# q computed transposed and unnormalised, with the root of its mean square moved into the scale of the sigmoids

## The chip, the cores and the metric

The kernel runs on one core of a Trainium2 chip, as one launch. The metric is the device time of that launch in microseconds (us). A core has a matrix engine (TensorE: PE, with its weight loads shown as PEld), a vector engine (VectorE: DVE), a scalar engine (ScalarE: ACT), a general engine (GpSimd: POOL) and a synchronisation engine (SyncE: SP), on which this program issues nearly all of its DMAs. Each engine works through its own list of instructions in order.

## The reference, cut to what matters

One layer of a streaming encoder, for 2048 tokens of width 1024. What touches the change is the attention branch: q, k and v are projections of the normalised input, q and k are normalised per head (8 heads of 64), and the scores' sigmoid is what the stick-breaking weights are made of.

```python
h = rms_norm(x, norm_g) * (1.0 + scale) + shift
u = h @ w_in
glu_in, gate_a, q, k, v, gate_b, m_a, m_b = jnp.split(u, IN_SPLITS, axis=-1)
...
q = q * lax.rsqrt(jnp.mean(q * q, axis=-1, keepdims=True) + EPS) * q_gain   # per head of 64
k = k * lax.rsqrt(jnp.mean(k * k, axis=-1, keepdims=True) + EPS) * k_gain
...
z = jnp.einsum("bqhd,bkhd->bhqk", qb, kb) * 64 ** -0.5
beta = sigmoid(z)                       # and 1 - beta = sigmoid(-z)
A[t, s] = beta[t, s] * prod_{s<j<t} (1 - beta[t, j])                        # s < t
o = A @ v
```

The other branch (a gated causal convolution of width 31 with a layer norm) and the gates, the output projections and the residual are the same before and after.

## The kernel before, in words

**Number format.** Every large product is made of three matmuls (`mm3`): each fp32 operand is split into a rounded part hi and a rest lo, and hi·hi, hi·lo and lo·hi are summed in PSUM.

**Stages.** The sequence is handled in 4 chunks of 512 tokens, in the order 3, 2, 1, 0 (the host has reversed it). The program has four stretches.

1. The opening (0 to about 166 us). The modulation columns are computed on DVE and ACT, x is loaded, normalised and transposed on PE into h^T (8 tiles of 128 channels by 512 tokens per chunk, hi and lo), chunk after chunk. The first chunk's q, k and v are computed here "at once", with weights and staging tiles out of a pool `hx` that lives only in the opening. SP's list in it holds the loads of w_ada, of the q, k and v weights and of x, and the stores of q, k and v, mixed.
2. The projections (to about 775 us): the other three chunks of q (group 0, then, after some gates, group 1), k and v; the GLU and the gates for all four chunks. A group is four heads. The convolution's taps are on a list `todo`, from which a few are emitted at each `tick()`; work that has to wait for other engines is put off by `later(n, ...)`, which runs it n ticks on.
3. The attention (to about 1520 us): 80 units (8 heads, and 10 pairs of a row chunk with a key chunk), each with four blocks of 128 queries. For each block: two z matmuls into PSUM, on ACT a sigmoid of z into w and one of -z back into z, on DVE a scan that multiplies up the sigmoids of -z, on POOL the product w. One unit later PE transposes w (four at a time), ACT copies the hi part and DVE subtracts the lo part, and PE multiplies by v. Between these, PE does the merge gates' matmuls as filler, at due times.
4. The output projections (to the end).

**Order.** The scheduler orders the instructions of each engine up to the end of q's group 0. From then on `pin[0]` is set, and PE's instructions (`mm`, `tr`) keep the order in which the program writes them, until the end of the attention.

**q and k before.** `nat_mm` (L215) takes h^T, 128 channels by 128 tokens, as the stationary operand and 256 columns of weights as the moving one: the result is q as tokens by channels, two such blocks in one PSUM tile `pd`, a half (two blocks) being 48 matmuls of 256 columns. ACT squares each head with an accumulator (L297; in the opening one Square for the half at L356 and a sum on DVE at L358). `head_norm` (L305) makes the root by three Newton steps on DVE and multiplies q by it into `qn` (L312). `transposed` (L318) turns `qn` on PE, four transposes for two heads (L123), into the PSUM tile `pt`; ACT writes hi (L331, for k with its gain L327), DVE lo (L332), and four DMAs on SP store them (L336, L337). The tiles `qhi` and `qlo` have one buffer each. k goes the same way with its own weights. In the attention `load_q` (L940) fetches q^T with three DMAs; `z_stage` (L948) multiplies and applies both sigmoids with the constants 1/8 and -1/8 as scale (L970, L971); `av_stage` (L991) transposes.

Of the kernel before, what the change touches and what calls it, by code (L numbers as in the profile page):

```python
# [8 lines left out]
F32 = mybir.dt.float32  # L9
# [42 lines left out]
def trunk_kernel(  # L52
# [105 lines left out]
    qst_d = [[dram(f"qst{h}_{g}", [P, CH], F32) for g in range(NCH)] for h in range(NH)]  # L158
    vst_d = [[dram(f"vst{h}_{g}", [P, 4, P], F32) for g in range(NCH)] for h in range(NH)]
# [40 lines left out]
    with ExitStack() as s1:  # L200
# [81 lines left out]
        def qk_group(grp, isk, chunks, w2=None):  # L282

            w2 = w2 or [piece(w_qkv[grp, i]) for i in range(2)]
            h4 = (grp % 2) * 4
            dst = kst_d if isk else qst_d
            for b in chunks:
# [14 lines left out]
                for pr in range(2):  # L302
                    later(3 + pr, lambda qn=qn, b=b, pr=pr: transposed(qn, pr, dst, h4, b, isk))
# [14 lines left out]
        def transposed(qn, pr, dst, h4, b, isk, pool=None):  # L318
# [5 lines left out]
            hi = (pool or cvp).tile([P, CH], F32R, tag="qhi", name="qhi", bufs=1)  # L324
            lo = (pool or cvp).tile([P, CH], F32R, tag="qlo", name="qlo", bufs=1)
            if isk:
                nc.scalar.mul(hi, ps, gain)  # L327
                nc.vector.scalar_tensor_tensor(out=lo, in0=ps, scalar=gain, in1=f(hi),
# [4 lines left out]
            for i in range(2):  # L333
                hd = slice(i * HD, (i + 1) * HD)
                dd = dst[h4 + 2 * pr + i][b]
# [14 lines left out]
        def norm_at_once(pss, grp, b, pool):  # L350
# [11 lines left out]
            for pr in range(2):  # L362
                transposed(qn, pr, kst_d if grp >= 2 else qst_d, (grp % 2) * 4, b, grp >= 2, pool)
# [36 lines left out]
        def h_chunk(g, pool, on_dve, xs=None, parts=4):  # L400
# [7 lines left out]
            for kc in range(KC):  # L408
# [3 lines left out]
                hf = pool.tile([P, CH], F32, tag="hf", name="hf", bufs=6)  # L412
# [8 lines left out]

        with tc.tile_pool(name="hx", reuse_waits="tile", bufs=1) as hx:
# [10 lines left out]
            def hf_tile():  # L433
                return hx.tile([P, CH], F32, tag="hf", name="hf", bufs=6)
# [30 lines left out]
            crow = [hx.tile([P, CH], F32, tag="hf", name="crow", bufs=6)[0:1] for _ in range(2)]  # L465
# [31 lines left out]
            qk_ps = [[pd.tile([P, 2, 256], F32, tag="pd", name="pd") for _ in range(2)]  # L497
# [13 lines left out]
            for kc in range(KC):  # L511
# [46 lines left out]

# [739 lines left out]
```

## Time and profile before

| what | value |
|---|---|
| time, median of 3 runs | 1840.88 us (1836.46 to 1841.89) |
| the profiled execution | 1840.99 us, its span 1839.3 us, granted clock 0.998 |
| busy over the span: PE, DVE, ACT, POOL | 1777.6, 1233.2, 833.5, 658.7 us |

| stretch (us) | length | PE busy | DVE busy | ACT busy | POOL busy |
|---|---|---|---|---|---|
| opening, first part, 0 to 20 | 20 | 6.66 | 9.06 | 7.99 | 0.75 |
| q of the first chunk, 20 to 55 | 35 | 30.23 | 29.49 | 21.40 | 3.18 |
| rest of the opening, 55 to 166 | 111 | 100.06 | 68.92 | 65.11 | 44.23 |
| projections, 166 to 775 | 609 | 606.51 | 435.36 | 163.99 | 128.73 |
| attention, 775 to 1520 | 745 | 720.94 | 571.00 | 537.51 | 466.34 |
| output projections, 1520 to 1839 | 319 | 313.19 | 119.42 | 37.48 | 15.44 |

The span is what the profile sees between its first and last instruction; the time has 1.7 us more around it. A busy time counts an engine's instructions as they overlap in its pipeline, once. In the lines of the trace, L12 is line 12 of the kernel, `x4` is a count, and an arrow `<-` at the end of a row says which work ended the idle time before it.

### The profile page before, as it was taken

To read this page: it belongs to the slowest core of one execution; us is meant where nothing else is said; L and a number is where in the kernel's file an instruction comes from. 1 tells how busy PE (TensorE), PEld (TensorE's weight loads), DVE (VectorE), ACT (ScalarE), POOL (GpSimd) and SP (SyncE) were. 2 spreads that over 40 slices of the span, in tenths; PEclk is the share of its full clock that TensorE was granted. 3 is DMA by queue.
4 is the path that set the end of the run, shared out by engine and by line. 5 is a ranking of instruction groups with operands and counts; after the bars stand their busy time and mean duration, and the time that the engine had idled before them with its cause. 6 is when DMAs were issued, how large, how long until landed. Compare 5 with 4: busy or idle time off the path is not lost.

```text
span 1839.3 us, 27219 instructions
## 1 busy us (share of the span) xinstructions
PE 1777.6 (97%) x9612; PEld 1510.2 (82%) x9612; DVE 1233.2 (67%) x1696; ACT 833.5 (45%) x1960; POOL 658.7 (36%) x819
## 2 busy tenths in 40 slices
PE   6899999999999999999999999999998899999999
PEld 5888889899898888878888888888776777888887
DVE  7645577987879565467778777877778785334341
ACT  5465113223131234367777777777777742010100
POOL 0253112102111233366666666666666721010100
PEclk9999999999999999999999999999999999999999
DMA  8563411415133453433232323232334336353532
GB/s 288 177 188 105 139 35 53 120 42 168 33 104 98 152 182 132 152 117 98 61 107 66 106 72 101 67 95 66 95 111 137 95 110 203 109 166 97 166 97 81
DMA packets 117597, 211.08 MB, mean 115 GB/s; under 512 B 15442, under 2 KB 27730, under 8 KB 117460
## 3 DMA queue, kind: packets, MB, share of 16 engines
q1 hardware_dynamic: 116308, 207.24, 36.2%
q10 hardware_dynamic: 1152, 2.10, 0.3%
q8 instruction: 76, 1.25, 0.3%
q14 instruction: 61, 0.50, 0.1%
HBM read 137.98 MB, written 71.30 MB: 114 GB/s over the span
## 4 chain that ended last, share of the span: by engine, by line
PE 75%; DVE 7%; DMA 5%; POOL 4%; issue 4%; ACT 4%; SPq 1%; DVEq 0%; ACTq 0%; POOLq 0%
PE pd L118 43%; PE po L118 8%; PE p L118 8%; PE av L118 5%; PE pT L123 5%; PE z L118 5%; POOL w L982 2%; DVE sc L975 2%; DVE tlo L1009 1%; DMA wl<-in_w_qkv_dram 1%; ACT z L971 1%; POOL wlo L106 1%; PE pt L123 1%; DMA qst<-qhi 1%; DMA xt<-in_x_n_dram 1%
## 5 line engine op out<-in xcount | busy, mean ns | idle before, releaser
L982 POOL TENSOR_TENSOR w<-w,sc 128x512 f32<-128x512 f32 (+1 forms) x320 | 361.3, 1130 | 243.0 <-DVE sc L975 177.5
L118 PE MATMUL pd<-hh,whi 128*128 128x512 f32 x1024 | 325.8, 399 | 0.0
L975 DVE TENSOR_TENSOR_SCAN sc<-z,sc,w 128x512 f32<-128x512 f32 x192 | 244.1, 1276 | 73.8 <-ACT z L971 72.2
L106 POOL TENSOR_TENSOR wlo<-wl,whi 128x512 fp32r<-128x512 f32 x88 | 130.9, 1499 | 409.4 <-ACT whi L105 408.4
L970 ACT ACTIVATE w<-z 128x512 f32<-128x512 f32 (+1 forms) x320 | 171.6, 536 | 128.9 <-PE z L118 102.9
L118 PEld LDWEIGHTS pd<-hh,whi 128*128 128x128 f32 x1024 | 184.2, 190 | 31.4
L118 PE MATMUL pd<-hhi,whi 128*128 128x512 f32 x512 | 208.5, 407 | 1.0 <-ACT vsg L882 1.0
L1009 DVE TENSOR_TENSOR tlo<-pT,thi 128x512 fp32r<-128x512 f32 (+1 forms) x320 | 185.8, 598 | 33.6 <-ACT thi L1008 30.5
L118 PE MATMUL pd<-hh,wlo 128*128 128x512 f32 x512 | 200.3, 391 | 0.0
L118 PE MATMUL pd<-hhi,wlo 128*128 128x512 f32 x512 | 200.2, 391 | 0.0
L118 PE MATMUL pd<-hlo,whi 128*128 128x512 f32 x512 | 200.2, 391 | 0.0
L118 PE MATMUL z<-kt,q 128*128 128x512 f32 (+2 forms) x640 | 190.5, 379 | 0.0
L123 PE MATMUL pT<-ident,w 128*128 128x128 f32 x1088 | 174.3, 274 | 11.9 <-POOL w L982 10.4
L1008 ACT CAST thi<-pT 128x512 fp32r<-128x512 f32 (+1 forms) x320 | 165.1, 526 | 42.6 <-PE pT L123 38.7
L123 PEld LDWEIGHTS pT<-ident,w 128*128 128x128 f32 x1088 | 136.8, 140 | 50.6 <-POOL w L982 18.6
L971 ACT ACTIVATE z<-z 128x512 f32<-128x512 f32 (+1 forms) x320 | 171.8, 537 | 0.0
L979 DVE TENSOR_TENSOR_SCAN sc<-z,tri 128x512 f32<-128x512 f32 (+3 forms) x128 | 103.9, 820 | 60.3 <-ACT z L971 40.6
L118 PE MATMUL av<-tlo,vt 128*128 128x512 f32 (+1 forms) x320 | 121.0, 378 | 11.1 <-DVE tlo L1009 10.4
L105 ACT CAST whi<-wl 128x512 fp32r<-128x512 f32 x88 | 53.6, 622 | 163.2 <-PE pd L118 135.5
L118 PEld LDWEIGHTS z<-kt,q 128*128 128x128 f32 x640 | 109.6, 189 | 14.6 <-DVE sc L979 0.3
L118 PE MATMUL av<-thi,vt 128*128 128x512 f32 (+1 forms) x320 | 116.7, 365 | 0.8 <-ACT thi L1008 0.8
L1116 ACT CAST yh<-ma 128x512 fp32r<-128x512 f32 x32 | 19.9, 621 | 206.4 <-DVE ma L1113 206.4
(289 smaller groups left out, 3641.2 us busy)
## 6 DMA issues: line engine op xcount, KB each, us to landing
wl<-in_w_in_dram SPq DMA_DIRECT2D x64, 256.0 KB, 2.9
wa<-in_w_ada_dram SPq DMA_DIRECT2D x24, 512.0 KB, 5.0
wl<-in_w_qkv_dram SPq DMA_DIRECT2D x36, 256.0 KB, 2.7
xt<-in_x_n_dram SPq DMA_DIRECT2D x16, 512.0 KB, 5.4
vst<-st SPq DMA_DIRECT2D x64, 128.0 KB, 1.9
kt<-kst SPq DMA_DIRECT2D x32, 256.0 KB, 3.1
vt<-vst SPq DMA_DIRECT2D x32, 256.0 KB, 2.7
q<-qst SPq DMA_DIRECT2D x32, 256.0 KB, 2.8
```

The source lines that it names most:

```text
L105: nc.scalar.copy(out=hi[:, s], in_=wl)
L106: (lo_eng or nc.gpsimd).tensor_tensor(out=lo[:, s], in0=wl, in1=f(hi[:, s]), op=ALU.subtract)
L118: i = nc.tensor.matmul(*a, **k)
L123: i = nc.tensor.transpose(*a)
L970: nc.scalar.activation(out=w[:, lo:], in_=z[:, lo:], func=AF.Sigmoid, scale=HD ** -0.5)
L971: nc.scalar.activation(out=z[:, lo:], in_=z[:, lo:], func=AF.Sigmoid, scale=-HD ** -0.5)
L975: nc.vector.tensor_tensor_scan(out=s[:, 1:], data0=z, data1=w, initial=s[:, 0:1], op0=ALU.mult, op1=ALU.bypass)
L979: nc.vector.tensor_tensor_scan(out=s[:, lo + 1:], data0=z[:, lo:], data1=tri[:, :CH - lo], initial=1.0, op0=ALU.mult, op1=ALU.max)
L982: nc.gpsimd.tensor_tensor(out=w[:, lo:], in0=w[:, lo:], in1=s[:, lo:CH], op=ALU.mult)
L1008: nc.scalar.copy(out=thi[:, :n], in_=pT[:, :n])
L1009: nc.vector.tensor_tensor(out=tlo[:, :n], in0=pT[:, :n], in1=f(thi[:, :n]), op=ALU.subtract)
L1116: nc.scalar.copy(out=hi, in_=ma)
```

## The change

q is computed as q^T: the weights (128 channels by 128 columns) are now the stationary operand, 512 tokens of h^T the moving one, so a half, which is now two heads and not two blocks of tokens, is 24 matmuls of 512 columns (`q_mm`). q^T is not normalised. `q_split` squares it on ACT into `sqv` (one buffer) and writes hi and lo straight from the PSUM tile. `q_sums` sums the squares over each head's 64 channels on PE: four fp32 matmuls per half, with 128 by 128 of the squares as the stationary operand and a 128 by 2 matrix `blk` of 1/64 as the moving one, into a PSUM tile `pss` from the pool of the transposes. `q_root` makes the root on DVE as before and writes it times 1/8 and times -1/8 into a tile `rq`, which is stored in DRAM. In the attention `load_q` fetches the part of `rq` for its head and row chunk (128 by 8) ahead of q^T, and both sigmoids take a column of it as their scale, one number for each of the 128 queries, in place of the constant. k keeps its method, its norm and its gain (which includes q's gain, before as after). In the opening hi and lo now come out of the 8 buffers of the tag `hf`, which had 6 and served h alone. The first `load_q` stands ahead of the attention's first filler.

```diff
+        def q_mm(ps, w2, half, b, kc):
+            o = (kc % 4) * 256 + half * P
+            wh, wl = (w[:, o:o + P] for w in w2[kc // 4])
+            mm3(ps, wh, wl, hT(b)[0][kc], hT(b)[1][kc], kc == 0, kc == KC - 1)
+
+        def q_split(ps, grp, half, b, pool, tag="qhi", bufs=1):
+            sq = pool.tile([P, CH], F32, tag="sg" if pool is not hx else "sqv", name="sqv", bufs=1)
+            nc.scalar.activation(out=sq, in_=ps, func=AF.Square)
+            hi_lo(ps, None, qst_d, (grp % 2) * 4 + 2 * half, b, pool)
+            return sq
+
+        def q_sums(sq, pss, half):
+            for t in range(4):
+                mm(pss[:, 4 * t + 2 * half:4 * t + 2 * half + 2], sq[:, t * P:(t + 1) * P], blk,
+                   start=True, stop=True)
+
+        def q_root(pss, grp, b):
...
+            r = rsqrt(sm, v, 16, "qr", keep=keep).rearrange("p (h t) -> p h t", h=4)
+            rq = qp.tile([P, 4, 2, 4], F32, tag="rq", name="rq", bufs=2)
+            for i, sign in enumerate((1, -1)):
+                keep(nc.vector.tensor_scalar(out=rq[:, :, i, :], in0=r,
+                                             scalar1=sign * HD ** -0.5, scalar2=None,
+                                             op0=ALU.mult))
+            nc.sync.dma_start(rq_d[grp][b], rq)
+
+        def q_group(grp, chunks, w2=None):
...
+            for b in chunks:
+                pss = []
+                for half in range(2):
+                    ps = pd.tile([P, CH], F32, tag="pd", name="pd")
+                    for kc in range(KC):
+                        q_mm(ps, w2, half, b, kc)
+                    sq = q_split(ps, grp, half, b, cvp)
+                    def sums(sq=sq, half=half, pss=pss, b=b):
+                        if not half:
+                            pss.append(pt.tile([P, CH], F32, tag="pt", name="pss"))
+                        q_sums(sq, pss[0], half)
+                        if half:
+                            q_root(pss[0], grp, b)
+                    later(1, sums)
+                    tick()
...
-            hi = (pool or cvp).tile([P, CH], F32R, tag="qhi", name="qhi", bufs=1)
-            lo = (pool or cvp).tile([P, CH], F32R, tag="qlo", name="qlo", bufs=1)
+            tags = ("hf", "hf", 8) if pool is hx else ("qhi", "qlo", 1)
+            hi = pool.tile([P, CH], F32R, tag=tags[0], name="qhi", bufs=tags[2])
+            lo = pool.tile([P, CH], F32R, tag=tags[1], name="qlo", bufs=tags[2])
...
-                        for i in range(2):
-                            nat_mm(ps2[half], w2, g0, half, i, kc,
-                                   kc == 0 and i == 0, kc == KC - 1 and i == 1)
+                        q_mm(ps2[half], w2, half, g0, kc)
...
+            def q_at_once(grp):
+                pss = pt.tile([P, CH], F32, tag="pt", name="pss")
+                for half in range(2):
+                    q_sums(q_split(qk_ps[grp][half], grp, half, g0, hx), pss, half)
+                q_root(pss, grp, g0)
...
-            norm_at_once(qk_ps[0], 0, g0, hx)
+            q_at_once(0)
...
         def load_q(h, rc):
+            rq = at.tile([P, 2, 4], F32, tag="rq", name="rq", bufs=2)
+            nc.sync.dma_start(rq, rq_d[h // 4][rc][:, h % 4])
...
-            nc.scalar.activation(out=w[:, lo:], in_=z[:, lo:], func=AF.Sigmoid, scale=HD ** -0.5)
+            nc.scalar.activation(out=w[:, lo:], in_=z[:, lo:], func=AF.Sigmoid,
+                                 scale=s_["rq"][:, 0, qb:qb + 1])
             nc.scalar.activation(out=z[:, lo:], in_=z[:, lo:], func=AF.Sigmoid,
-                                 scale=-HD ** -0.5)
+                                 scale=s_["rq"][:, 1, qb:qb + 1])
```

The order of the instructions moves at three places. In the rows below the arrow goes from the operands to the result, the shape behind it is that of the result, and `x4` counts rows that are alike.

The first is PE in q's group 1, where PE keeps the program's order. Before, at the point where one chunk's matmuls pass into the next (`hhi` and `hlo` are h^T, `whi` and `wlo` the weights, the second operand moves):

```order
L118 MATMUL pd<-wlo,hhi_0_1717 128x256
L118 MATMUL pd<-whi,hlo_0_1725 128x256
L123 MATMUL pt<-ident,qn 128x128 x4
L118 MATMUL pd<-whi,hhi_0_1710 128x256
L118 MATMUL pd<-wlo,hhi_0_1710 128x256
L118 MATMUL pd<-whi,hlo_0_1718 128x256
```

After, at the end of the first half of a chunk (`hh` holds hi and lo of a chunk together):

```order
L118 MATMUL pd<-hh_334,whi 128x512 x2
L118 MATMUL pd<-hh_334,wlo 128x512
L118 MATMUL pss<-blk,sqv 128x2 x4
L118 MATMUL pd<-hh_327,whi 128x512 x2
L118 MATMUL pd<-hh_327,wlo 128x512
```

The four transposes, which stood at least a tick behind the work that they read, are gone; the four sums of a half stand directly behind that half's last matmul, and read what ACT makes of its result.

The second is SP at the end of the opening, where the last chunk of x is loaded. Before (`vst` is the store of v, `xt` a tile of 128 tokens of x, and `ca` is c for the modulation's third part):

```order
L348 DMA vst_3_154<-st 128x256
L348 DMA vst_3_158<-st 128x256
L348 DMA vst_3_162<-st 128x256
L348 DMA vst_3_166<-st 128x256
L373 DMA xt<-in_x_n_dram 128x1024 x4
L597 DMA ca<-in_c_dram 128x1024
```

After:

```order
L408 DMA vst_3_162<-st 128x256
L408 DMA vst_3_166<-st 128x256
L408 DMA vst_3_170<-st 128x256
L408 DMA vst_3_174<-st 128x256
L250 DMA wa<-in_w_ada_dram 128x1024 x2
L433 DMA xt<-in_x_n_dram 128x1024 x4
L667 DMA ca<-in_c_dram 128x1024
```

Two loads of the gate's columns of w_ada, of 512 KB each, now stand ahead of the four loads of x; they go into the buffers out of which the v stores read.

The third is SP in the middle of the opening, where the first chunk's q of group 1 is stored (`qst`, chunk 3) and the v weights (`wl`) are fetched. Before:

```order
L336 DMA qst_3_122<-qhi 64x512
L336 DMA qst_3_126<-qhi 64x512
L337 DMA qst_3_122<-qlo 64x512
L337 DMA qst_3_126<-qlo 64x512
L104 DMA wl<-in_w_qkv_dram 128x512
L336 DMA qst_3_130<-qhi 64x512
L336 DMA qst_3_134<-qhi 64x512
L104 DMA wl<-in_w_qkv_dram 128x512
L337 DMA qst_3_130<-qlo 64x512
L337 DMA qst_3_134<-qlo 64x512
```

After:

```order
L397 DMA qst_3_126<-qlo 64x512
L396 DMA qst_3_130<-qhi 64x512
L397 DMA qst_3_130<-qlo 64x512
L396 DMA qst_3_134<-qhi 64x512
L397 DMA qst_3_134<-qlo 64x512
L315 DMA rq_3_142<-rq 128x32
L104 DMA wl<-in_w_qkv_dram 128x512 x2
L433 DMA xt<-in_x_n_dram 128x1024 x2
L104 DMA wl<-in_w_qkv_dram 128x512 x2
```

The q stores of the group stand together ahead of the weights, with the store of `rq` behind them, where before they stood among them.

In the attention the order on PE and DVE is that of before; SP has the 32 loads of `rq` more.

More of the change, by code (lines that the diff above doesn't have):

```diff
@@ L158, in trunk_kernel @@
     qst_d = [[dram(f"qst{h}_{g}", [P, CH], F32) for g in range(NCH)] for h in range(NH)]
+    rq_d = [[dram(f"rq{i}_{g}", [P, 4, 2, 4], F32) for g in range(NCH)] for i in range(2)]
     vst_d = [[dram(f"vst{h}_{g}", [P, 4, P], F32) for g in range(NCH)] for h in range(NH)]
@@ new lines, in q_sums @@
+        def q_sums(sq, pss, half):
[3 more added lines that the diff above has]
+        def q_root(pss, grp, b):
+            v = sm.tile([P, 16], F32, tag="qv", name="qv")
+            keep(nc.vector.tensor_scalar(
+                out=v.rearrange("p (h t) -> p h t", h=4),
+                in0=pss[:, :16].rearrange("p (t h) -> p h t", h=4),
+                scalar1=EPS, scalar2=None, op0=ALU.add))
+            r = rsqrt(sm, v, 16, "qr", keep=keep).rearrange("p (h t) -> p h t", h=4)
[5 more added lines that the diff above has]
+            nc.sync.dma_start(rq_d[grp][b], rq)
@@ L285, in qk_group, with k_group @@
+        def k_group(grp, chunks):
+            w2 = [piece(w_qkv[grp, i]) for i in range(2)]
             h4 = (grp % 2) * 4
-            dst = kst_d if isk else qst_d
             for b in chunks:
@@ L323, in transposed, with hi_lo @@
                     qn[:, t, 2 * pr:2 * pr + 2, :].rearrange("p h d -> p (h d)"), ident)
-            hi = (pool or cvp).tile([P, CH], F32R, tag="qhi", name="qhi", bufs=1)
-            lo = (pool or cvp).tile([P, CH], F32R, tag="qlo", name="qlo", bufs=1)
-            if isk:
-                nc.scalar.mul(hi, ps, gain)
-                nc.vector.scalar_tensor_tensor(out=lo, in0=ps, scalar=gain, in1=f(hi),
+            hi_lo(ps, gain, kst_d, h4 + 2 * pr, b, pool)
+        def hi_lo(ps, by, dst, h, b, pool):
+            tags = ("hf", "hf", 8) if pool is hx else ("qhi", "qlo", 1)
+            hi = pool.tile([P, CH], F32R, tag=tags[0], name="qhi", bufs=tags[2])
+            lo = pool.tile([P, CH], F32R, tag=tags[1], name="qlo", bufs=tags[2])
+            if by is not None:
+                nc.scalar.mul(hi, ps, by)
+                nc.vector.scalar_tensor_tensor(out=lo, in0=ps, scalar=by, in1=f(hi),
                                                op0=ALU.mult, op1=ALU.subtract)
@@ L420, in h_chunk @@
                     yield
+        blk = qp.tile([P, 2], F32, name="blk", bufs=1)
+        nc.gpsimd.memset(blk, 0.0)
+        for i in range(2):
+            nc.gpsimd.memset(blk[i * HD:(i + 1) * HD, i:i + 1], 1.0 / HD)
+        hx = None
         with tc.tile_pool(name="hx", reuse_waits="tile", bufs=1) as hx:
@@ L433, in hf_tile @@
             def hf_tile():
-                return hx.tile([P, CH], F32, tag="hf", name="hf", bufs=6)
+                return hx.tile([P, CH], F32, tag="hf", name="hf", bufs=8)
             def wa_load(j):
@@ L464, in trunk_kernel @@
             w2_q1 = [hx_tiles("w1") for _ in range(2)]
-            crow = [hx.tile([P, CH], F32, tag="hf", name="crow", bufs=6)[0:1] for _ in range(2)]
+            crow = [hx.tile([P, CH], F32, tag="hf", name="crow", bufs=8)[0:1] for _ in range(2)]
             for i in range(2):
@@ L496, in trunk_kernel @@
                                      op0=ALU.add, op1=ALU.mult)
-            qk_ps = [[pd.tile([P, 2, 256], F32, tag="pd", name="pd") for _ in range(2)]
+            qk_ps = [[pd.tile([P, CH], F32, tag="pd", name="pd") for _ in range(2)]
                      for _ in range(2)]
@@ L957, in z_stage @@
                     nxt = (h, rc + 1) if rc + 1 < NCH else (h + 1, 0)
-                    for hr in ((h, rc), nxt) if n_ == 0 else (nxt,):
-                        if hr[0] < NH:
-                            load_q(*hr)
+                    if nxt[0] < NH:
+                        load_q(*nxt)
             s_ = st[h, rc]
@@ L1153, in trunk_kernel @@
         psum = lambda n: pd.tile([P, CH], F32, tag="pd", name=n)
+        load_q(0, 0)
         while nf < PRE:
```

24 lines of the change are left out of this document (12 added, 12 removed).

## The prediction, made before the result was known

> **What bounds the kernel now.** I read first the page's head: how long, and which engine is full.
>
> ```profile
> span 1839.3 us, 27219 instructions
> PE 1777.6 (97%) x9612; PEld 1510.2 (82%) x9612; DVE 1233.2 (67%) x1696; ACT 833.5 (45%) x1960; POOL 658.7 (36%) x819
> ```
>
> PE is busy for 97% of the span, so there are some 60 us in which anything but PE's own work could set the time. Where these lie is told by the busy time of each engine in the stretches of the program (columns: stretch, length, then busy time of PE, PEld, DVE, ACT, POOL, the granted clock, the DMA share and GB/s):
>
> ```profile
> 20.00:55.00 35.00, 30.23 (x215) 29.31 (x216) 29.49 (x49) 21.40 (x43) 3.18 (x2) 0.95 0.69 241
> 55.00:166.00 111.00, 100.06 (x802) 96.38 (x801) 68.92 (x167) 65.11 (x170) 44.23 (x37) 0.98 0.51 157
> 166.00:775.00 609.00, 606.51 (x3431) 533.08 (x3429) 435.36 (x567) 163.99 (x511) 128.73 (x88) 1.00 0.35 110
> 775.00:1520.00 745.00, 720.94 (x3775) 589.70 (x3776) 571.00 (x721) 537.51 (x1167) 466.34 (x674) 1.00 0.31 95
> ```
>
> From 166 to 775 us PE idles 2.5 of 609 us: there a PE instruction more or less is time lost or won, and nothing that DVE or ACT are spared counts. In the attention PE idles 24 of 745 us, with ACT at 72%; in the opening, from 20 to 166 us, 4.8 + 10.9 = 15.7 us. The change touches all three. What ends PE's idle time in the attention is in the table of waits (engine, tile, line, what it waited for; us in all, times, longest):
>
> ```profile
> PE pT L123 <- POOL w L982: 10.4, 11, 2.6
> PE av L118 <- DVE tlo L1009: 10.4, 22, 1.6
> ...
> PEld av L118 <- DVE tlo L1009: 25.1, 41, 1.9
> PEld pT L123 <- POOL w L982: 18.6, 33, 2.9
> ```
>
> Both waits come by way of ACT: POOL's w needs the scan of the sigmoid, and tlo needs ACT's copy, which stands in one list with the sigmoids. The rows of PEld say that more weight loads than matmuls come late, and that PE has work left for part of them.
>
> **The matmuls.** A half of q is now 24 matmuls of 512 columns in place of 48 of 256. The chain of waits (start, us, what) has both kinds, and the transposes:
>
> ```profile
> 306.64 5.74 PE pd L118 x48
> 312.38 0.44 PE pt L123 x4
> ...
> 1574.25 43.52 PE p L118 x192
> ```
>
> The first row is the half of one chunk: 5.74 us, or 0.120 each. The last is 512 columns wide: 43.52 / 192 = 0.2267 each, so 24 take 5.44. That is -0.30 a half, and over 16 halves (8 chunk-groups: two groups, four chunks) -4.8 us, of which -3.6 in the 12 halves after the opening and -1.2 in the opening. The Trainium skill, "TensorE: Matmul & The Clock Gate", section "Back-to-back issue gap", puts the isolated spacing at 109 ns for 256 columns and 216 for 512; by it a half would win 48 x 0.109 - 24 x 0.216 = 0.05 us, under 1 us in all, and the sum below would be some 4 us higher. The trace's 256-wide row has 11 ns over that figure, its 512-wide one 11 too, so the narrow form pays its overhead twice as often; I go by the rows.
>
> Two times four transposes go per chunk-group, 0.88 us by the middle row, over 8 of them -7.0: -5.3 after the opening, -1.8 in it.
>
> **The sums.** The trace has no such matmul, but the layer norm's sums are of the same kind: fp32, a stationary operand of 128 by 128, a moving one of one column, eight instructions for four sums. PE's timeline where they stand between 512-wide ones (start, us, what):
>
> ```profile
> 685.78 0.39 PE L118 MATMUL pd<-hh,wlo 128*128 128x512 f32 x1
> ...
> 686.01 0.95 PE L118 MATMUL pst<-invc,t 128*128 128x1 f32 x8
> ...
> 686.82 0.71 PE L118 MATMUL pd<-hh,whi 128*128 128x512 f32 x2
> ...
> 687.36 0.39 PE L118 MATMUL pd<-hh,wlo 128*128 128x512 f32 x1
> ```
>
> From their start to that of the next matmul is 0.81 us, and the next two take 0.54 where two take 0.45: four sums cost 0.90. Two moving columns in place of one are hardly more. Times 16: +14.4, of which +10.8 after the opening and +3.6 in it. The bounds: nothing where PE would idle anyway, and 0.95, the busy time of the eight, if none of it overlaps.
>
> Matmuls, transposes and sums together: -3.6 - 5.3 + 10.8 = **+1.9** after the opening, -1.2 - 1.8 + 3.6 = **+0.6** in it. What was to be saved on PE is spent on PE.
>
> **A new wait.** In group 1 the sums follow their half's matmuls directly, and read squares that ACT makes only when the half is done; behind the sums on PE stand the next half's matmuls, which wait with them. What ACT's square takes and when it may start is shown by a sigmoid of the same shape behind the matmul that ends at 685.78 + 0.39 = 686.17:
>
> ```profile
> 686.21 0.60 ACT L871 ACTIVATE vsg<-pd 128x512 f32<-128x512 f32 x1 [0.31 <-PE pd L118]
> ...
> L356 ACT ACTIVATE sqv<-pd 128x512 f32<-128x512 f32 x8 | 4.8, 595 | 11.3 <-PE pd L118 7.2 <-DVE qry L95 3.4 <-DVE ssq L358 0.8
> ...
> 685.56 0.19 PEld L118 LDWEIGHTS pd<-hh,wlo 128*128 128x128 f32 x1
> ```
>
> 0.04 to start, 0.60 for the square (the opening's squares average 0.595), 0.19 for the first weight load, which nothing covers any more: 0.83 us, and with ACT busy 27% of this stretch now and then something stands before it: 0.9. Six halves make **+5.4**. In group 0 the scheduler has put the sums between other matmuls; the last halves have less between, and the square has one buffer, so I take two of the six, **+1.8**. Ends: 0 (all covered) and 12 x 0.9 = 10.8. What DVE and ACT are spared here (the multiplication by the root, squares by head, the wait for the norm) lies under 606.5 us of PE and is worth nothing.
>
> **The opening.** PE's waits from 55 to 160 us, all of them but small ones, then the rows from which the queue is priced:
>
> ```profile
> PE pd L118 <- POOL whx L106: 3.8, 5, 1.9
> PE pt L123 <- DVE xt L389: 2.9, 3, 1.3
> PE pd L118 <- ACT whx L105: 1.8, 2, 0.9
> PE pt L123 <- DVE qn L312: 1.8, 1, 1.8
> PE pd L118 <- POOL u L665: 0.6, 1, 0.6
> ...
> SPq L336 <- ACT qhi L331: 5.9, 3, 4.3
> ...
> 131.47 1.86 SPq L373 DMA_DIRECT2D xt<-in_x_n_dram  x4
> ...
> 131.91 4.63 DMA xt<-in_x_n_dram
> ...
> wa<-in_w_ada_dram SPq DMA_DIRECT2D x24, 512.0 KB, 5.0
> ...
> vst<-st SPq DMA_DIRECT2D x64, 128.0 KB, 1.9
> ```
>
> For the better: q's norm is gone (the 1.8 behind `qn`), and q's stores no longer wait for the single `qhi` (SP stood 5.9 us there with the k and v weights behind it, for which PE waited 3.8 + 1.8). I count the first in full and half of the others: 1.8 + 2.8 = 4.6 won. For the worse: two loads of w_ada, which wait until the v stores have left their buffer (1.9), are issued (1.86 / 4 = 0.47 each) and take bandwidth (1 MB; by 512 KB in 5.0 with four under way, some 2.5 us) ahead of the last chunk's x, whose landing is on the chain now, at 4.63 us: 1.9 + 0.9 + 2.5 = 5.3 lost. These cancel: **0**, with ends of -10.9 (every wait of the table goes) and +9 (nothing won, 5.3 lost, and the four halves' sums wait 0.9 for their square).
>
> **The attention.** The trace has no sigmoid whose scale is a column. The nearest is k's copy with the gain, next to q's without it:
>
> ```profile
> L327 ACT ACTIVATE qhi<-pt,gain 128x512 fp32r<-128x512 f32 x16 | 11.2, 701 | 6.1 <-DMA kst<-qhi 5.0 <-DVE cb L634 1.0
> L331 ACT CAST qhi<-pt 128x512 fp32r<-128x512 f32 x16 | 9.8, 610 | 11.8 <-DMA qst<-qhi 9.1 <-DVE qn L312 1.4 <-PE pt L123 1.3
> ...
> L970 ACT ACTIVATE w<-z 128x512 f32<-128x512 f32 x224 | 134.5, 601 | 107.1 <-PE z L118 90.8 <-PE pT L123 10.0 <-POOL sc L988 2.0
> L971 ACT ACTIVATE z<-z 128x512 f32<-128x512 f32 x224 | 134.9, 602 | 0.0
> ...
> 1103.13 0.60 ACT L970 ACTIVATE w<-z 128x512 f32<-128x512 f32 x1 [1.04 <-PE z L118]
> 1103.63 0.59 ACT L971 ACTIVATE z<-z 128x512 f32<-128x512 f32 x1
> ```
>
> 701 against 610 ns: +0.09 each, and that is what I give all 640 sigmoids, whose fixed part doesn't depend on their width: +58 us of ACT's time, 537.5 to 596 of 745, or 80%. A pair runs back to back (starts 0.50 apart), so a block's second result comes 2 x 0.09 = 0.18 later. PE meets this where it already waits: 11 + 22 waits of PE make 33 x 0.18 = 6, the 33 + 41 of its weight loads 74 x 0.18 = 13. I take **+10**, nearer the second since a late load is what turns into a late matmul. The ends are 0 (the 24 us in which PE idles are not on one chain, and filler lies between) and +58 (ACT's list becomes the bound). The 32 loads of `rq` stand one unit ahead of their use, 745 / 80 = 9.3 us, and q's own loads beside them cost PE no wait; +0, and if that cover failed, one small DMA's flight each time, by the 1.9 of v's stores up to 32 x 1.9 = 61.
>
> **The sum**: 0.6 + 1.9 + 5.4 + 1.8 + 0 + 10 = 19.7, on the profiled execution's 1840.99 (0.1 above the median): **1860.7 us**.
>
> **The rivals.**
>
> *The attention hides the longer sigmoids.* For it: ACT has 28% left, and PE 24 us idle; the program places filler between a block and its use. Against: 33 waits on the very chain. Without the 10, and with the opening's 4.6 won and x's loss covered by h's work: 0.6 + 1.9 + 7.2 - 4.6 = +5.1, **1846**, at the edge of what can be told.
>
> *Faster: the opening is set by its chain, not by PE.* Place: from 20 to 166 us, where q's squares, root, multiplication, transposes and copies in a single buffer stood between PE and the k and v weights. If all of PE's 15.7 us of idle time there goes, with the attention at 0: 0.6 + 1.9 + 7.2 - 15.7 = -6.0, **1835**. It decides as soon as the opening wins more than the 9.7 that PE's work and the squares cost plus what the attention takes. For it: four of the five waits in the table are of its kind. Against: the w_ada loads ahead of x, and one wait removed usually uncovers the next.
>
> *ACT becomes the bound of the attention.* Every unit's eight sigmoids push ACT's copies of pT back, tlo with them, and PE's next product: all 58 us, or at least 40 of them, show: 9.7 + 40 to 58, **1891 to 1909**. For it: ACT's list is in order, and PE waits on tlo more often than on anything. Against: its idle time before L970 is 107 us, most of it for PE's z, so half of that must be used up first.
>
> *That nothing moves*: if the squares were covered (0), the opening even and the sigmoids hidden, only +2.5 is left, **1843.5**; I count it with the first.
>
> **How the numbers follow.** My forecast, +10 to +35, has 0.60; the first rival (with the last) 0.16, faster 0.14, ACT as the bound 0.10. A measurement of this kernel can tell 0.3%, or 5.5 us, from no change: 1835.4 to 1846.4. Faster: 0.10 of the 0.14 and 0.03 of the first rival, 0.13. The same: 0.04 of the faster, 0.10 of the first rival, 0.01 of the forecast, 0.15. Slower: 0.72. The range reaches down to 1838 (it leaves out 0.13) and up to 1888 (0.07 beyond, of ACT as the bound), which takes in the attention at 0 with the squares at their full price and the attention at +35 with the opening at 0; the forecast's own is 1851 to 1876.
>
> **What would show it.** In the profile after: 24 matmuls in 5.4 us on the chain; `pss` rows of about 0.8 us; PE waits on ACT's `sqv` in 8 or so halves of 0.7 to 0.9 us each, none if I am wrong; the stretch from 166 to 775 us longer by 9 us; the sigmoids at 690 to 700 ns, ACT at 590 to 600 us between 775 and 1520, and the waits on L982's and L1009's successors up by some 10 us. The forecast is wrong if the sigmoids stay at 600 ns, if the attention's length does not move, or if x's last tiles land as early as before and the opening is shorter by 10 us or more.

## The result, and the profile after

The changed kernel takes 1851.12 us (median of 6 runs, 1848.66 to 1852.35) where the kernel before takes 1840.93 (6 runs, 1836.46 to 1842.52): 10.2 us slower, a ratio of 1.0055 with a 95% interval of 1.0044 to 1.0066. The forecast was 1860.7, 19.7 above the profiled execution: the direction was right, the size was twice what came; 1851.1 is the lower end of the forecast's own 1851 to 1876. Two executions, one of the kernel before at 1969.28 us and one of the three edits together at 2254.12 us, ran at granted clocks of 0.85 and 0.73 and are left out (with the second, the median of the three edits would be 1834.11).

The head of the page of the changed kernel:

```profile
span 1848.8 us, 26472 instructions
PE 1786.1 (97%) x9292; PEld 1495.1 (81%) x9292; DVE 1225.1 (66%) x1692; ACT 865.2 (47%) x1780; POOL 661.0 (36%) x822
```

PE has 320 instructions fewer and is busy 8.5 us longer. Fewer, wider matmuls and no transposes of q brought no net saving on PE, as the sum had it. Where the 9.5 us of the span lie is told by five moments that both programs have: the fifth sigmoid of the GLU (the first of its second block, shortly before q's group 1), the ninth (behind group 1), the attention's first z matmul, its last av matmul, and the end. Their starts are read from the timelines, the differences are the lengths (us):

| stretch | before | after | difference | forecast |
|---|---|---|---|---|
| start to the fifth GLU sigmoid (opening, q's group 0) | 239.4 | 243.4 | +4.1 | +3.4 |
| to the ninth (q's group 1) | 102.6 | 109.6 | +7.1 | +6.4 |
| to the first z (rest of the projections) | 443.0 | 441.0 | -2.0 | 0 |
| to the last av (attention) | 722.1 | 724.0 | +1.9 | +10 |
| to the end | 332.3 | 330.8 | -1.5 | 0 |

The forecast's column splits the prediction's sum by the same moments: 0.6 + 0.95 + 1.8 + 0 in the first row, 0.95 + 5.4 in the second. The first two rows are within a microsecond; the attention is not. Lengths of single executions vary by some 2 us: the last stretch is 330.6 to 333.3 us long in the runs below other than the first two, though they change nothing in it, and the attention 722.2 to 724.3 in the eight profiled executions that have the changed kernel's.

**Group 1.** PE's timeline of the changed kernel where one half passes into the next (start, us, what, and in brackets the idle time ahead):

```profile
293.85 0.39 PE L118 MATMUL pd<-hh,wlo 128*128 128x512 f32 x1
294.99 1.05 PE L118 MATMUL pss<-blk,sqv 128*128 128x2 f32 x8 [0.75 <-ACT sqv L292]
295.90 0.49 PE L118 MATMUL pd<-hhi,whi 128*128 128x512 f32 x1
296.23 0.40 PE L118 MATMUL pd<-hlo,whi 128*128 128x512 f32 x1
...
302.39 1.05 PE L118 MATMUL pss<-blk,sqv 128*128 128x2 f32 x8 [0.75 <-ACT sqv L292]
```

Four sums are eight instructions on PE, as the layer norm's are, and PE stands 0.75 us for ACT's square ahead of them. The sums of the next half start at 302.39, 7.40 us on. 24 matmuls alone are 5.44: a half pays 1.96 for sums and stall, where 1.8 was forecast, and PE has seven such waits in the program, 5.2 us:

```profile
PE pss L118 <- ACT sqv L292: 5.2, 7, 0.7
```

**The attention.** The sigmoids by shape, and what PE waited for there:

```profile
L1041 ACT ACTIVATE w<-z,rq 128x512 f32<-128x512 f32 x224 | 156.0, 697 | 85.8 <-PE z L118 59.4 <-PE pT L123 7.7 <-POOL w L1056 7.1
L1043 ACT ACTIVATE z<-z,rq 128x512 f32<-128x512 f32 x224 | 150.4, 671 | 0.0
...
PE pT L123 <- POOL w L1054: 13.6, 23, 2.6
PE av L118 <- DVE tlo L1081: 5.9, 20, 1.0
...
PEld av L118 <- DVE tlo L1081: 23.7, 49, 1.4
PEld pT L123 <- POOL w L1054: 22.5, 35, 2.9
```

The price of a column was near the forecast's 0.09: 601 to 697 ns for the first sigmoid of a pair, 602 to 671 for the second, and ACT's busy time in the attention rises by 45 us, from 532 to 578. What it does to PE was not. The waits on POOL's w went from 11 to 23 and by 3 us, those on tlo by 4.5 us the other way: together 20.8 before and 19.5 after. The late weight loads, which the forecast had leaned on, are 84 in place of 74, and 46.2 us in place of 43.7.

**The opening.** The last chunk of x is issued as late as before, but lands far later, as SP's timeline and the chain of waits show:

```profile
130.11 1.65 SPq L250 DMA_DIRECT2D wa<-in_w_ada_dram  x2
131.80 2.16 SPq L433 DMA_DIRECT2D xt<-in_x_n_dram  x4
...
129.47 1.84 DMA vst<-st
131.43 0.33 SPq L250
...
133.23 9.06 DMA xt<-in_x_n_dram
```

Before, the piece of x on the chain took 4.63 us from its issue to its landing; now it takes 9.06. The two loads of w_ada cost time on the queue and in flight. The second of them is issued at 131.43, when a v store has landed (129.47 + 1.84 = 131.31), and x behind it: 1.9 us after the last v store's issue is done (129.93). That x is issued only 0.3 us later than before is because the v stores end 1.4 us earlier. In the run with x first (below) x follows the v stores by 0.1 us:

```profile
124.52 4.49 SPq L410 DMA_DIRECT2D vst<-st  x8
129.11 1.85 SPq L435 DMA_DIRECT2D xt<-in_x_n_dram  x4
```

Its four loads of x land 3.7 to 6.5 us after their issue (median 5.4), those of the changed kernel 6.7 to 9.1 (median 7.9). So by these two executions some 1.8 us were lost on the queue and 2.5 in flight.

### The profile page after: what moved, and what is told of

The parts are those of the page before. It is cut to its first block, busy times and chain, and to the rows that moved or that the text cites. A ratio compares the mean times of both kernels' runs of the same rounds, so it can differ in the third digit from the quotient of the medians.

```text
span 1848.8 us, 26472 instructions
## 1 busy us (share of the span) xinstructions
PE 1786.1 (97%) x9292; PEld 1495.1 (81%) x9292; DVE 1225.1 (66%) x1692; ACT 865.2 (47%) x1780; POOL 661.0 (36%) x822
## 4 chain that ended last, share of the span: by engine, by line
PE 71%; DVE 10%; POOL 6%; ACT 4%; issue 4%; DMA 4%; SPq 0%; DVEq 0%; POOLq 0%; ACTq 0%
PE pd L118 41%; PE po L118 9%; PE p L118 8%; PE pT L123 4%; PE av L118 4%; POOL w L1054 4%; PE z L118 3%; DVE sc L1047 3%; DVE tlo L1081 2%; DMA wl<-in_w_qkv_dram 1%; ACT z L1043 1%; DVE sc L1051 1%; ACT thi L1080 1%; ACT w L1041 1%; PE pss L118 1%
## 5 line engine op out<-in xcount | busy, mean ns | idle before, releaser
L118 PE MATMUL pd<-hh,whi 128*128 128x512 f32 x1120 | 358.0, 400 | 3.7 <-ACT hh L134 1.9
L1041 ACT ACTIVATE w<-z,rq 128x512 f32<-128x512 f32 (+1 forms) x320 | 202.4, 633 | 102.4 <-PE z L118 68.4
L118 PE MATMUL pd<-hhi,whi 128*128 128x512 f32 x576 | 234.1, 406 | 1.0 <-ACT vsg L952 1.0
L118 PE MATMUL pd<-hlo,whi 128*128 128x512 f32 x576 | 226.0, 392 | 1.0 <-POOL hlo L478 1.0
L118 PE MATMUL pd<-hhi,wlo 128*128 128x512 f32 x576 | 225.5, 391 | 0.0
L118 PE MATMUL pd<-hh,wlo 128*128 128x512 f32 x560 | 219.0, 391 | 0.0
L1043 ACT ACTIVATE z<-z,rq 128x512 f32<-128x512 f32 (+1 forms) x320 | 193.7, 605 | 0.0
L118 PEld LDWEIGHTS pd<-hhi,wlo 128*128 128x128 f32 x576 | 108.3, 188 | 23.1
L118 PEld LDWEIGHTS pd<-hhi,whi 128*128 128x128 f32 x576 | 109.4, 190 | 19.9 <-ACT vsg L952 1.4
L118 PEld LDWEIGHTS pd<-hlo,whi 128*128 128x128 f32 x576 | 108.7, 189 | 20.2 <-POOL hlo L478 2.1
```

Source lines behind the costliest of these rows:

```text
L118: i = nc.tensor.matmul(*a, **k)
L1041: nc.scalar.activation(out=w[:, lo:], in_=z[:, lo:], func=AF.Sigmoid, scale=s_["rq"][:, 0, qb:qb + 1])
L1043: nc.scalar.activation(out=z[:, lo:], in_=z[:, lo:], func=AF.Sigmoid, scale=s_["rq"][:, 1, qb:qb + 1])
```

## The experiments

Twelve kernels were run. Each is given with its edit, and its lengths in the table's stretches where they bear on the verdict.

### The longer sigmoids alone, first try

The kernel before, with a constant column as scale:

```diff
+    eighth = cp.tile([P, 2], F32, name="eighth")
+    for i, sign in enumerate((1, -1)):
+        nc.gpsimd.memset(eighth[:, i:i + 1], sign * HD ** -0.5)
...
-            nc.scalar.activation(out=w[:, lo:], in_=z[:, lo:], func=AF.Sigmoid, scale=HD ** -0.5)
+            nc.scalar.activation(out=w[:, lo:], in_=z[:, lo:], func=AF.Sigmoid, scale=eighth[:, 0:1])
...
-                                 scale=-HD ** -0.5)
+                                 scale=eighth[:, 1:2])
```

> The kernel before, with both sigmoids of the attention taking their scale from a column (a constant 1/8 and -1/8 for every query) and nothing else changed: the price of the longer sigmoid by itself. Theory (ACT had the room): sigmoids 0.07 to 0.10 us longer each, ACT's busy time between 785 and 1508 us up by 45 to 60 us from 533, the attention longer by 0 to 3 us from 723.3, the time 0 to 3 us above the kernel before. Rival (the waits on w and tlo each grow by the two sigmoids, and the changed kernel hid that for another reason): +6 to +13 us.

And with a bias column of zeros as well (`eighth` has three columns, `bias=eighth[:, 2:3]` in both):

> As the run before, and the sigmoids also take their bias from a column (zeros): the suspected cost doubled. Theory (hidden as long as ACT has room and PE has filler): the sigmoids 0.15 to 0.2 us longer than in the kernel before, ACT at 620 to 650 of 723 us, the time 2 to 12 us above the kernel before, more than twice the run before since the room runs out. Rival (the cost is proportional, from the waits that PE already had): exactly twice what the run before costs. Third (a bias column costs nothing beside a scale column): ACT as in the run before, and the time too.

Measured: 1848.64 us, a ratio of 1.0042 (1.0030 to 1.0055), so 8.1 us slower, and 1855.76, 1.0079 (1.0065 to 1.0093), 15.2 us slower. By the times alone the rival had won, and proportionally. The stretches say otherwise. In the first of the two the attention is 724.9 us long, 2.8 more than before, and the last stretch 5.4 more. The chain of waits of that run, in the output projections:

```profile
1578.87 43.52 PE p L118 x192
1622.39 44.64 PE po L118 x192
```

In the kernel before both kinds of 192 matmuls take 43.52. The new tile of 8 bytes a partition moved the tiles behind it. Contrary to what the next expectation says, it did not move the resident output weights: these lie in a pool on the other side (`wor`, `side="right"`) and have the same address in both programs, while the tiles of y, which they are multiplied with, lie 32 bytes further on. Of the 192 matmuls the 168 with the resident weights became 6.7 ns longer each (some 395 in place of 390 ns busy); the 24 with the first piece of the weights, which moved along with y, did not. So the place of the tiles makes the difference; which rule is behind it is not shown. No sigmoid runs in the output projections: the experiment had measured its own scaffolding.

### The longer sigmoids alone, nothing moved

The same two, with the columns in a tile that the program has anyway and does not use:

```diff
-    ctx.enter_context(tc.tile_pool(name="rp", bufs=1, side="right")).tile([P, 72], F32, name="skew")
+    eighth = ctx.enter_context(tc.tile_pool(name="rp", bufs=1, side="right")).tile(
+        [P, 72], F32, name="skew")
+    for i, value in enumerate((HD ** -0.5, -HD ** -0.5)):
+        nc.gpsimd.memset(eighth[:, i:i + 1], value)
```

> The first run on the longer sigmoid once more, the constant columns now in a tile that the program has anyway, so that no other tile changes its place (there, the eight bytes of the new tile moved the output weights, and 192 matmuls with them took 44.64 us in place of 43.52). Theory (ACT had the room): the attention 723 to 725 us long with ACT at 575 to 580, the output stage back at 291.0, the time 0 to 3 us above the kernel before. Rival (the sigmoids themselves cost the 8 us that the first run showed): +6 to +10, with the output stage still long or the attention 728 and more.

> As the run before, with a bias column (zeros) beside the scale column: the cost of the sigmoids doubled. Theory (a threshold: the room on ACT runs out between 80% and 87%): the attention 729 to 732 us long, ACT at 625 to 630, the output stage 291, the time 6 to 10 us above the kernel before, well over twice the run before. Rival (proportional): twice what the run before costs, within 1 us. If most of the first runs' cost was the place of the tiles in the attention too: under +4.

Measured: 1841.76 us, 1.0005 (0.9996 to 1.0014), not to be told from no change, with the attention at 722.3; and 1847.68, 1.0041 (1.0026 to 1.0055), 7.1 us slower, with the attention at 729.6. The sigmoids and PE's waits in the stretch from 775 to 1520 us, first of the run with the scale column, then of the one with both:

```profile
L973 ACT ACTIVATE w<-z,skew 128x512 f32<-128x512 f32 x224 | 156.1, 697 | 85.1 <-PE z L121 76.1 <-PE pT L126 7.4
...
775.00:1520.00 745.00, 722.94 (x3777) 588.89 (x3776) 569.54 (x721) 583.37 (x1166) 467.13 (x673) 1.00 0.31 95
PE pT L126 <- POOL w L986: 12.8, 22, 2.7
PE av L121 <- DVE tlo L1013: 6.4, 21, 1.0
```

```profile
L973 ACT ACTIVATE w<-z,skew 128x512 f32<-128x512 f32 x224 | 176.8, 789 | 55.8 <-PE z L121 47.9 <-PE pT L126 3.2 <-PE av L121 1.6
...
775.00:1520.00 745.00, 716.79 (x3740) 582.21 (x3741) 569.57 (x712) 636.00 (x1165) 469.27 (x674) 1.00 0.31 94
PE pT L126 <- POOL w L986: 19.7, 36, 1.9
PE av L121 <- DVE tlo L1013: 5.2, 21, 0.4
```

The first column costs ACT 46 us and the program nothing; the second costs ACT 53 more (the stretch is cut at fixed times, so both are a little off) and the program 6 to 7. So the cost is not in proportion to the sigmoids' length: it begins somewhere between the two. The first run has nearly the same waits as the changed kernel (22 and 21 times, 12.8 and 6.4 us), so these are the sigmoids' doing there too. From the second column on the waits on w grow without a counterpart.

### The changed kernel with constant scales

```diff
-                                 scale=s_["rq"][:, 0, qb:qb + 1])
+                                 scale=HD ** -0.5)
...
-                                 scale=s_["rq"][:, 1, qb:qb + 1])
+                                 scale=-HD ** -0.5)
```

> The changed kernel with the constants 1/8 and -1/8 as the sigmoids' scale again; it leaves out q's normalisation in the scores, all else (squares, sums, root, its loads) is done. Theory (all but about 2 us of the change's cost lies before the attention): 1848 to 1851 us, attention 723 to 725 us, ACT back to 533. Rival (the sigmoids cost 10 us and something else in the attention won 8): 1841 us, attention 715.

Measured: 1849.17 us (1846.30 to 1850.12), 2.0 below the changed kernel, the attention 721.5 us where that has 724.0 (1.5 less than expected). From both sides, then, the sigmoids' share of the 10 us is 0 to 2.5 us.

### The sums a tick later

```diff
-            sq = pool.tile([P, CH], F32, tag="sg" if pool is not hx else "sqv", name="sqv", bufs=1)
+            sq = pool.tile([P, CH], F32, tag="sg" if pool is not hx else "sqv", name="sqv",
+                           bufs=2 if pool is not hx else 1)
...
-                    later(1, sums)
+                    later(2, sums)
...
-                    sg = cvp.tile([P, CH], F32, tag="sg", name="sg", bufs=1)
+                    sg = cvp.tile([P, CH], F32, tag="sg", name="sg", bufs=2)
```

(`rq` has one buffer in place of two, for the room.)

> The changed kernel with each half's four sums put one tick later (behind the next half's matmuls), and two buffers in place of one for the squares and the gates' sigmoid that share their tag. Theory (PE stands 0.7 us and a bare weight load for the square in each half of group 1): the waits of pss on sqv, 5.2 us in 7 cases, are gone, a half's period in group 1 falls from 7.40 to 6.4 us, the time 5 to 7 us below the changed kernel, 1844 to 1846. Rival (PE is late there by its own work, or the wait moves to the next user of ACT): no more than 2 us won, 1849 to 1851.

Measured: 1846.07 us, 5.0 below the changed kernel, 1.0030 (1.0020 to 1.0041) against the one before. Group 1 is 103.3 us in place of 109.6, and PE's timeline has no wait at the sums any more:

```profile
300.87 0.39 PE L118 MATMUL pd<-hhi,wlo 128*128 128x512 f32 x1
301.09 0.95 PE L118 MATMUL pss<-blk,sqv 128*128 128x2 f32 x8
301.90 0.48 PE L118 MATMUL pd<-hhi,whi 128*128 128x512 f32 x1
...
307.43 0.95 PE L118 MATMUL pss<-blk,sqv 128*128 128x2 f32 x8
```

A half is 6.34 us: 5.44 and 0.90 for the sums, the forecast's figure to the digit. So the 1.96 was 0.90 of sums and 1.06 of stall, the stall 6.4 us in all (5.4 was forecast). In this profiled execution the opening was 2.5 us longer than the changed kernel's, with the granted clock at 0.83 from 20 to 40 us.

### The sums in the rounded format

```diff
-            sq = pool.tile([P, CH], F32, tag="sg" if pool is not hx else "sqv", name="sqv", bufs=1)
+            sq = pool.tile([P, CH], F32R, tag="sg" if pool is not hx else "sqv", name="sqv", bufs=1)
...
+        blk = qp.tile([P, 2], F32R, name="blk", bufs=1)
+        nc.gpsimd.tensor_copy(blk, blk_)
```

> The changed kernel with the squares and the 1/64 matrix in the rounded format of the other matmuls, so that a sum is one pass over PE in place of two. Theory (the sums' 0.9 us a half is PE's own work and on its path in all 16 halves): pss groups of 0.4 to 0.5 us, each half 0.4 to 0.5 shorter, the time 4 to 7.5 us below the changed kernel, 1843.5 to 1847. Rival (in the opening and where PE stands for the square they are covered): only 2 us or less. The wait for sqv stays in both.

Measured: 1842.72 us, 8.4 below the changed kernel, 1.0013 (1.0004 to 1.0022) against the one before. The sums in group 1:

```profile
297.43 0.61 PE L118 MATMUL pss<-blk,sqv 128*128 128x2 f32 x4 [0.75 <-ACT sqv L292]
297.89 0.48 PE L118 MATMUL pd<-hhi,whi 128*128 128x512 f32 x1
```

Four instructions in place of eight, 0.46 us to the next matmul in place of 0.91, the stall as it was: group 1 is 2.7 us shorter (6 x 0.45), the stretch ahead of it 4.1 (10 halves x 0.45 is 4.5). The sums are on PE's path in the opening as well; nothing covers them. The total is 0.9 us more than expected; 1.3 of it lies in the attention, which the edit does not touch, within what its length varies by.

### No sums

`q_sums` does nothing, and the root is taken of ones:

```diff
-                mm(pss[:, 4 * t + 2 * half:4 * t + 2 * half + 2], sq[:, t * P:(t + 1) * P], blk,
-                   start=True, stop=True)
...
+            keep(nc.vector.memset(v, 1.0))
```

> The changed kernel without the 64 sums of squares, with the root taken of ones: it leaves out q's norm, while the squares, the root, its stores and loads and the longer sigmoids stay. Theory (the sums with their stall are what makes the new form no gain, 14.4 and some 5 to 7 us as forecast): group 1's stage 109.6 - 6 x 1.9 = 98 us, so 4 to 5 below that of the kernel before (102.6), and the time 17 to 21 below the changed kernel, 1830 to 1834. Rival (part of the sums is covered, above all in the opening): group 1 the same, the time 12 to 15 below, 1836 to 1839.

Measured: 1826.84 us (1826.33 to 1828.98), 0.9925 (0.9912 to 0.9937) against the kernel before: 24 us below the changed kernel. Group 1 is 97.9 us long, 11.7 less than with the sums (1.95 a half) and 4.7 less than before the change; the stretch ahead of it is 231.6, 11.9 less. The rest of the projections (440.9) and the attention (723.2) are within a microsecond of the changed kernel's. So matmuls and transposes were saved as forecast (in group 1: 6 x 0.30 + 3 x 0.88 = 4.4 forecast, 4.7 measured), and the sums with their wait took all of it there and 7 us more. In group 1 the first theory holds; the total is 3 us beyond its bound. In the stretch ahead ten halves at 0.90 and one wait of some 1.1 make 10.1; the other 1.8 us are not located.

### x ahead of w_ada

The loads of w_ada are held behind the last load of x on SP:

```diff
+                last_x[:] = [order(nc.sync.dma_start(
+                    xs[i], x_n[(tb0 + i) * P:(tb0 + i + 1) * P, :]))]
...
-                nc.sync.dma_start(wa, w_ada[j])
+                with tc.issue_after(last_x[0].ins):
+                    nc.sync.dma_start(wa, w_ada[j])
```

> The changed kernel with the loads of w_ada for the gate held behind the last load of x on SP, as they stood before the change, nothing else moved. Theory A (the two loads ahead of x delay the last chunk and with it the opening by 3 to 5 us): 1846 to 1848.5 us, the first sigmoid of the gates at 173 to 175 in place of 178.2. Theory B (x's last tiles land under other work of PE, which has no more idle time after 100 us than before): no change, 1850 to 1852.

Measured: 1847.48 us, 3.6 below the changed kernel, 1.0033 (1.0020 to 1.0046) against the one before. The stretch up to the fifth GLU sigmoid is 239.2, that of the kernel before (239.4). Theory A: the term of 5.3 us lost to these loads was real, and some 4 in size.

### The single tiles again

Beside x ahead of w_ada, q's and k's parts in the opening in the single tiles of before:

```diff
-            tags = ("hf", "hf", 8) if pool is hx else ("qhi", "qlo", 1)
+            tags = ("qhi", "qlo", 1)
```

(and `hf` with 6 buffers).

> The run with x's loads first, and in the opening the single tiles qhi and qlo for q's and k's parts in place of the eight buffers of hf (which has six again): that part of the change undone. Theory (SP stood 5.9 us for qhi with the k and v weights behind it, and PE waited 5.6 us for those): the opening 2 to 4 us longer than with x first (174.0), the time 1849 to 1852. Rival (the q stores of the changed kernel stand at another place in SP's list, and PE's waits for whx were 3.2 us with eight buffers too): within 1.5 us of the run with x first, 1847.5.

Measured: 1842.45 us (11 runs, 1840.21 to 1845.04), 1.0011 (1.0002 to 1.0020) against the kernel before: 5.0 below the run with x first, where 2 to 4 more were expected. Both expectations are wrong. SP's waits from 20 to 170 us, first with eight buffers, then with one (L389 and L393 are ACT's copies for k and for q, L104 the loads of the weights):

```profile
SPq L104 <- POOL whx L106: 30.2, 12, 10.3
...
SPq L398 <- ACT qhi L393: 8.5, 5, 3.2
```

```profile
SPq L104 <- POOL whx L106: 21.6, 10, 4.6
...
SPq L398 <- ACT qhi L393: 6.4, 6, 2.6
SPq L398 <- ACT qhi L389: 6.1, 2, 4.4
```

With one tile SP does wait longer for qhi (12.5 us against 8.5), but shorter for the staging buffers of the weights (21.6 against 30.2): with eight buffers the wait that was taken away comes back as a longer one behind it. But that is SP's time and not PE's: PE waits 5.4 us for whx with eight buffers and 4.5 with one (from 20 to 175 us), 0.9 of the 5.0. The profiled execution of this run has only 1.7 us of the 5.0 in the opening (237.6 against 239.2), and is itself longer than the median; the rest is not located. So it is shown that the single tiles are faster here, and not why. By the order of instructions, the single tiles put x's loads ahead of those of w_ada even without the hold, so the order that cost 3.6 us came with the eight buffers.

### The edits together

The three edits that won (a tick later, rounded, x first):

> The changed kernel with the three edits together that were run apart: the sums a tick later (won 5.0 us), the loads of w_ada behind x (3.6), the sums in the rounded format (8.4). Theory (they act at different places, and only the sums' own time in group 1 is counted twice if the stall went with it): 1834 to 1838 us, so 2 to 6 us below the kernel before, with group 1's half at 5.9 us and no wait on sqv. Rival (they overlap, since all three end in the same opening or the clock there falls): 1839 to 1843, no better than before.

Measured: 1833.93 us, 0.9969 (0.9956 to 0.9982): faster than the kernel before by 6.5 us. Group 1 is 100.9 us long, a half 5.94, and no wait on sqv is left. The three add up: 5.0 + 8.4 + 3.6 = 17.0, measured 17.2. With the single tiles as the fourth:

> The three edits together (1834.1 us) and the opening's single tiles qhi and qlo again, which won 5 us beside x's loads first. Theory (the eight buffers let ACT and SP run ahead with work that nothing waits for, whatever the sums do): 1828 to 1831. Rival (in the three together the opening is already shorter, 169.9 to its end in place of 174.0, so the same time cannot be won twice): 1833 to 1835.

Measured: 1832.50 us (1828.98 to 1834.97), 0.9958 (0.9945 to 0.9972), 8.5 us below the kernel before. The fourth edit brought 1.4 of its 5.0, and the median lies between the two expectations. The five executions spread over 6 us; the profiled one is the fastest of them and has 5.0 us less in the stretch to the fifth GLU sigmoid (230.2 against 235.2). So it is not settled which holds. By its median this is the fastest version that computes q's norm.

## Why the prediction was right, and where it was not

**What bounds the kernel** was right: from 166 to 775 us every PE instruction counts, and what DVE and ACT were spared there was worth nothing.

**Matmuls, transposes, sums.** 5.44 us for 24 matmuls, 0.90 for four sums: both as worked out from rows of the kernel before, one by a matmul of the same shape, the other by the nearest kind (the layer norm's sums). The run without sums shows the saving (4.7 us in group 1), the late sums the price (6.34 - 5.44 = 0.90). By the isolated spacing that the Trainium skill gives ("TensorE: Matmul & The Clock Gate", section "Back-to-back issue gap") the matmuls would have won an estimated 0.05 us a half, and group 1 without its sums 6 x 0.05 + 3 x 0.88 = 2.9; the measured 4.7 stands with the rows.

**The new wait** was there, in 7 cases where 8 were named, at 1.06 us a half in place of 0.9. Of these 0.75 are idle time by the row; that the rest is the weight load and the first pass of the sums, which have nothing under them, is argued and not shown.

**The opening** came out as 0 by two terms, of which one was right and one was of the wrong sign. Lost to the loads of w_ada: 5.3 forecast (2.8 on the queue, 2.5 of bandwidth), 3.6 measured by the run with x first; the two traces show 1.8 on the queue and 2.5 in flight. Won by the eight buffers: 2.8 forecast, and the single tiles turned out 5 us better. The step that failed here is "q's stores no longer wait for the single qhi", with half of PE's 3.8 + 1.8 us of waiting for whx put down to it. In the changed kernel these waits of PE are 3.2 us, which looks like the forecast; but with x first they are 5.4 with eight buffers and 4.5 with one, and SP, which stands less for qhi (8.5 against 12.5), stands longer for the staging buffers of the weights, which POOL sets free (30.2 against 21.6). The order that put w_ada ahead of x came with the eight buffers too. What makes them slower beyond that stays open. That the opening's total came near the forecast is chance to that extent.

**The attention** is the term that made the forecast twice too large: +10 forecast, +1.9 in the profile, and +0.9 us (by the interval of its ratio -0.7 to +2.6) in the run that has nothing else. Without that term the sum is 9.7, or 1850.7 us. The duration (0.09 each, 58 us of ACT) was near, 45 measured. By the forecast's own sign ("if the attention's length does not move") this term is wrong. The step that failed is the product of the number of waits and the delay of a pair: it takes each of PE's 33 or 74 waits as the end of a chain that starts at the sigmoids and has no room in it. The row on which the prediction could have weighed this was quoted there: 107 us of idle time on ACT ahead of the first sigmoid, most of it for PE's own z. After the change it is 86. ACT was waiting for PE, so a longer sigmoid first used up some of that, and PE lost time only in the run whose bias column brought it down to 56. That this room is what decides is read from the three rows; no run varied it by itself. The third rival had this argument; the forecast did not apply it to itself. The first rival, that the attention hides the longer sigmoids, was right on its mechanism, and the result lies between its 1846, which counts an opening won, and the forecast.

**Not foreseen**: -2.0 us in the later projections. The kernel before has a wait there that the changed one has not, a single row of its timeline:

```profile
621.25 1.21 PE L118 MATMUL pd<-whi,hh 128*128 128x256 f32 x8 [1.75 <-DVE sg L693]
```

It is not that DVE's list is shorter now: ahead of that multiplication, which starts at 620.51, DVE stands idle for 4.95 us in the kernel before, and for 4.96 in the changed one ahead of the same multiplication at 631.73. There PE's next matmuls start without it, at 630.56. Why they no longer wait for it is not shown.

## What to carry to other kernels

A wait of the bounding engine is not a price list for a longer instruction ahead of it: ask first for whom the lengthened engine itself waits, since time in which it waits for the bound is room (here ACT's idle time, 190 us of the attention's 722, took 46 us of longer sigmoids for next to nothing, and twice that cost 7 us). Fewer and wider matmuls are worth only what the helper products do not take back; four small fp32 products cost PE as much as four matmuls of 512 columns (0.90 and 0.91 us), and where they read what another engine makes of the product just done, put a block of other work between. In an experiment, see that no other tile changes its place: eight bytes more a partition cost more than the thing that was to be measured.

## What the runs showed of the hardware

- **The place of a tile.** With a tile of 8 bytes a partition more in the program, groups of 192 matmuls with the output weights take 44.64 us in place of 43.52 (232.5 ns each for 226.7), at the same clock of 1.00 and with no wait; with the same sigmoids and no such tile they take 43.52.
- **A column as operand of an activation** of 128 by 512: scale, 601 to 697 ns for the first and 602 to 671 for the second of a pair; bias on top, 697 to 789 and 672 to 764. The Trainium skill, "ScalarE: Activation LUTs", section "What ACT_TABLE_LOAD costs", gives some 93 ns for each such operand; the first of a pair agrees (96 and 92), the second, back to back, is 69 to 70 for the scale and 92 for the bias.
- **A sum of two columns** on PE: eight instructions and 0.91 us for four products in fp32, four and 0.46 us in the rounded format, with 128 by 128 stationary.
- **The granted clock in the opening** differs between profiled executions at the same place: from 80 to 100 us it was 0.83 in the changed kernel and 0.91 in the one with constant scales, whose opening is the same, and from 20 to 40 us 1.00 in the changed kernel and 0.83 in the run with late sums. Differences of 2 us in the opening of single profiled executions are therefore not explained here by the edits; verdicts on it rest on the medians.
